# Storing the last 528 columns of the last tile in fifteen partition blocks of falling size

## Chip, cores, metric

One core of a Trainium2 chip runs the kernel. The metric is the device time of one execution in microseconds (us). A profiled execution also has a span, from its first to its last instruction, which is some 1.8 us shorter than the time; all points in time below count from the start of the span.

## The reference

```
x: (8, 4096, 2112) float32
pooled    = x.reshape(8, 1024, 4, 2112).mean(axis=2)
upsampled = repeat(pooled, 4, axis=1)
return x - upsampled
```

Every group of four neighbouring rows loses its mean. 277 MB are read and 277 MB written.

## The kernel before

A tile is 128 groups: 128 partitions with 4 x 2112 = 8448 columns of float32, so 33,792 B per partition. There are n = 64 tiles and six slots of buffer. SyncE issues the loads, VectorE does three adds and one fused multiply-add, ACT issues the stores.

```
for k in range(n):
    b, lap = k % SLOTS, k // SLOTS
    ...
    load = nc.sync.dma_start(out=slots[b][:], in_=xg[tile_rows])
    if lap:
        load._wait_ge(store_sems[b], 16 * lap)
    load.then_inc(load_sems[b], 16)
    ...                                   # three adds into s, then rows += -1/4 * s
    store = nc.scalar.dma_start(out=og[tile_rows], in_=slots[b][:])
    store._wait_ge(done_sem, done)
    store.then_inc(store_sems[b], 16)

for b in range(SLOTS):
    nc.sync.wait_ge(store_sems[b], 16 * len(range(b, n, SLOTS)))
```

Each of the 128 DMAs of this kernel leaves sixteen packets of 4 bytes (2048 in all), one at the end of its rows on each of the sixteen DMA engines; I call them *closing packets*. The semaphore of the last tile's slot shows 176 updates for its eleven stores, sixteen each, so a closing packet adds one. I call the moment at which the semaphore shows it the *increment*: the last closing packet comes at 1282.991 us, its increment at 1283.337. The two are recorded apart.

## Time and profile before

| | before |
|---|---|
| time | 1286.78 us (1286.73 to 1287.18, 6 runs) |
| span | 1285.0 us |
| VectorE busy | 1026.5 us, 80% |
| moved | 553.67 MB, 431 GB/s over the span |
| last store: issued / last closing packet / last increment | 1269.60 / 1282.99 / 1283.34 us |

From the page of the kernel before, the DMA queues (packets, MB, share of sixteen engines) and the issues (KB each, median us to landing):

```profile
q1 hardware_dynamic: 9216, 276.83, 50.0%
q10 hardware_dynamic: 9216, 276.83, 49.9%
q14 instruction: 2, 0.02, 0.0%
...
slot<-in_x_dram SPq DMA_DIRECT2D x64, 4224.0 KB, 59.7
out_dram<-slot ACTq DMA_DIRECT2D x64, 4224.0 KB, 43.9
```

Queue q1 carries the loads, q10 the stores. Most of a store's life here is spent in the queue: it takes 10.0 us of the engines' time (eight rows of 1247 ns on each) and lands 43.9 us after its issue (median).

### The profile page before, as it was taken

To read this page: it belongs to the slowest core of one execution; us is meant where nothing else is said; L and a number is where in the kernel's file an instruction comes from. 1 tells how busy PE (TensorE), PEld (TensorE's weight loads), DVE (VectorE), ACT (ScalarE), POOL (GpSimd) and SP (SyncE) were. 2 spreads that over 40 slices of the span, in tenths; PEclk is the share of its full clock that TensorE was granted. 3 is DMA by queue.
4 is the path that set the end of the run, shared out by engine and by line. 5 is a ranking of instruction groups with operands and counts; after the bars stand their busy time and mean duration, and the time that the engine had idled before them with its cause. 6 is when DMAs were issued, how large, how long until landed. Compare 5 with 4: busy or idle time off the path is not lost.

```text
span 1285.0 us, 439 instructions
## 1 busy us (share of the span) xinstructions
DVE 1026.5 (80%) x256; POOL 0.2 (0%) x4
## 2 busy tenths in 40 slices
DVE  5998778787787877878778788787887878878774
POOL 0000000000000000000000000000000000000000
DMA  9999999999999999999999999999999999999998
GB/s 404 421 438 432 426 438 437 430 429 437 437 431 429 437 437 431 429 437 437 431 429 437 437 431 429 437 436 430 430 438 434 429 432 438 434 428 433 438 434 374
DMA packets 18434, 553.67 MB, mean 431 GB/s; under 512 B 2048, under 2 KB 2048, under 8 KB 2048
## 3 DMA queue, kind: packets, MB, share of 16 engines
q1 hardware_dynamic: 9216, 276.83, 50.0%
q10 hardware_dynamic: 9216, 276.83, 49.9%
q14 instruction: 2, 0.02, 0.0%
HBM read 276.82 MB, written 276.82 MB: 431 GB/s over the span
## 4 chain that ended last, share of the span: by engine, by line
DVE 80%; another core or an unknown queue 17%; DMA 1%; issue 0%; SPq 0%
DVE slot L75 45%; DVE s_ps L71 12%; DVE s_sb L71 12%; DVE s_ps L66 6%; DVE s_sb L66 6%; DMA slot<-in_x_dram 1%; SPq L118 0%; SPq L53 0%
## 5 line engine op out<-in xcount | busy, mean ns | idle before, releaser
L75 DVE SCALAR_TENSOR_TENSOR slot<-s_sb,slot 128x8448 f32<-128x8448 f32 x32 | 286.7, 8958 | 1.1
L75 DVE SCALAR_TENSOR_TENSOR slot<-s_ps,slot 128x8448 f32<-128x8448 f32 x32 | 286.6, 8957 | 1.1
L66 DVE TENSOR_TENSOR s_sb<-slot 128x2112 f32<-128x2112 f32 x32 | 75.5, 2358 | 123.4 <-DMA slot<-in_x_dram 123.4
L66 DVE TENSOR_TENSOR s_ps<-slot 128x2112 f32<-128x2112 f32 x32 | 75.7, 2367 | 113.0 <-DMA slot<-in_x_dram 113.0
L71 DVE TENSOR_TENSOR s_ps<-s_ps,slot 128x2112 f32<-128x2112 f32 x64 | 151.4, 2366 | 2.2
L71 DVE TENSOR_TENSOR s_sb<-s_sb,slot 128x2112 f32<-128x2112 f32 x64 | 150.9, 2358 | 2.2
L107 POOL MEMSET const-uint8-127<- 128x1 uint8 x1 | 0.1, 102 | 0.0
L107 POOL MEMSET const-bfloat16-1.0<- 128x1 bf16 x1 | 0.1, 101 | 0.0
L107 POOL MEMSET const-float32-0.0<- 128x1 f32 x1 | 0.1, 98 | 0.2 <-issue 0.2
L107 POOL MEMSET const-float32-1.0<- 128x1 f32 x1 | 0.1, 98 | 0.0
## 6 DMA issues: line engine op xcount, KB each, us to landing
slot<-in_x_dram SPq DMA_DIRECT2D x64, 4224.0 KB, 59.7
out_dram<-slot ACTq DMA_DIRECT2D x64, 4224.0 KB, 43.9
```

Source lines behind the costliest of these rows:

```text
L66: add = nc.vector.tensor_add(out=s[:], in0=rows[:, 0, :], in1=rows[:, 1, :])
L71: add = nc.vector.tensor_add(out=s[:], in0=s[:], in1=rows[:, f, :])
L75: sub = nc.vector.scalar_tensor_tensor(out=rows, in0=s[:, None, :].to_broadcast([P, STRIDE, D]), scalar=-1.0 / STRIDE, in1=rows, op0=mybir ...
L107: nc = _bacc.Bacc("TRN2", target_bir_lowering=False, num_devices=1)
```

## The change

The intent is to balance the sixteen DMA engines at the end: a block of s < 16 partitions is meant to put one row on each of the first s engines, so blocks of falling size give the first engines more short rows than the last. That the engines are taken in a fixed order is an assumption, and the trace doesn't number them. I count them in that order: engine j is the one that a block of j + 1 partitions reaches and a block of j does not.

```diff
+EDGE = 528
+BLOCKS = (15, 14, 13, 12, 11, 10, 9, 9, 8, 7, 6, 5, 4, 3, 2)
...
-            store = nc.scalar.dma_start(out=og[tile_rows], in_=slots[b][:])
+            split = W - EDGE if k == n - 1 else W
+            store = nc.scalar.dma_start(
+                out=og[tile_rows, :split], in_=slots[b][:, :split]
+            )
...
-        for b in range(SLOTS):
-            nc.sync.wait_ge(store_sems[b], 16 * len(range(b, n, SLOTS)))
+        last = (n - 1) % SLOTS
+        p0 = 0
+        for size in BLOCKS:
+            store = nc.scalar.dma_start(
+                out=og[G - P + p0:G - P + p0 + size, W - EDGE:],
+                in_=slots[last][p0:p0 + size, W - EDGE:],
+            )
+            store.then_inc(store_sems[last], 16)
+            p0 += size
+        assert p0 == P
+
+        for k in range(n - SLOTS, n):
+            extra = len(BLOCKS) if k == n - 1 else 0
+            nc.sync.wait_ge(store_sems[k % SLOTS], 16 * (k // SLOTS + 1 + extra))
```

## The prediction

> **What bounds the kernel now.** I read the page first, for the engine that is full. Columns of the slice view: each digit is the busy share of one fortieth of the span.
>
> ```profile
> DVE 1026.5 (80%) x256; POOL 0.2 (0%) x4
> ...
> DMA  9999999999999999999999999999999999999998
> GB/s 404 421 438 432 426 438 437 430 429 437 437 431 429 437 437 431 429 437 437 431 429 437 437 431 429 437 436 430 430 438 434 429 432 438 434 428 433 438 434 374
> ...
> HBM read 276.82 MB, written 276.82 MB: 431 GB/s over the span
> ```
>
> The DMA row is full from the first slice to the last, VectorE is idle a fifth of the time. So the sixteen DMA engines bound the kernel, and only the last slice (374 GB/s) has room. The waits agree: VectorE waits for loads alone, and SyncE, which issues the loads, waits for stores (first answer VectorE's, second SyncE's):
>
> ```profile
> DVE s_sb L66 <- DMA slot<-in_x_dram: 123.4, 30, 13.3
> DVE s_ps L66 <- DMA slot<-in_x_dram: 113.0, 30, 4.8
> ...
> SPq L61 <- DMA out_dram<-slot: 1170.2, 58, 50.6
> SPq L92 <- DMA out_dram<-slot: 89.3, 1, 89.3
> ```
>
> The last line is the end of the program: SyncE waits 89.3 us for the last store. The change touches that store only, so I cut the tail into windows (us; VectorE busy; POOL; clock; DMA share; GB/s; a packet is counted in the window where it starts):
>
> ```profile
> 1253.00:1270.00 17.00, 16.06 (x4) 0.00 (x0) 1.00 0.97 419
> 1270.00:1280.50 10.50, 0.00 (x0) 0.00 (x0) 1.00 1.06 457
> 1280.50:1281.00 0.50, 0.00 (x0) 0.00 (x0) 1.00 0.16 68
> 1281.00:1281.40 0.40, 0.00 (x0) 0.00 (x0) 1.00 0.01 0
> 1281.40:1281.80 0.40, 0.00 (x0) 0.00 (x0) 1.00 0.21 85
> 1281.80:1283.00 1.20, 0.00 (x0) 0.00 (x0) 1.00 0.00 0
> ```
>
> 85 GB/s over 0.40 us is 34 kB: one row of 33,792 B starts there, and nothing after it. The packet records give the rest: a full row takes an engine 1247 ns from start to start (27.1 GB/s). Fifteen engines write the closing semaphore packet between 1281.200 and 1281.747; the sixteenth starts its last row at 1281.744 and closes at 1282.991. **One engine ends 1.24 us after the next.** The semaphore shows its increment at 1283.337.
>
> Why that one is late is in the records too. The page has two small packets on the instruction queue (q14 instruction: 2, 0.02 MB). They lie at 205.70 and 845.42 us, 8192 B each, and both times the same engine's stream falls back: a 302 ns gap, then a row of 1788 ns instead of 1251, so 0.84 us. Twice that is 1.68 us. On the lists of landings the last of the sixteen lags the fifteenth by about 0.1 us before the first fetch, 0.4 to 0.5 us between them, 1.23 to 1.39 us after the second. 8192 B are 128 instructions [...], and VectorE issues four per tile: 32 tiles at 20 us are the 640 us between the fetches, so I take them for VectorE's instructions. **The trace doesn't number the DMA engines**, so which one this is I can't read from it. The answer hangs on that.
>
> [...] The kernel before has only 128-partition DMAs and sixteen closing packets for each (2048 for 128 DMAs)[...]. [...] The trace shows 8 KiB pieces and that the fetch isn't free for the data.[...] Here the increment shows 0.34 us after the last packet, and rows behind a closing packet start at once[...].
>
> **The change, part by part.** The generated order is the same except for fifteen more DMA issues on the ACT queue and a different order of the closing waits.
>
> 1. The last store loses 528 of 8448 columns: 2112 B a row, by rate 1247 x 2112/33792 = 78 ns. Each engine has eight rows: 0.62 us less on every engine.
> 2. Blocks 15, 14, 13, 12, 11, 10, 9, 9, 8, 7, 6, 5, 4, 3, 2 give engines 0 to 15 this many short rows: 15, 15, 14, 13, 12, 11, 10, 9, 8, 6, 5, 4, 3, 2, 1, 0 (sum 128). A short row is 78 ns, its closing packet about 6 ns (9982 ns between the closing packets of two stores, less 8 x 1247): 84 ns. Net, after step 1: engines 0 and 1 +0.64 us, engine 7 +0.13, engine 8 +0.05, engine 11 -0.29, engine 15 -0.62.
> 3. Fifteen issues more. The first six loads, issued back to back, took 2.94 us, 0.49 each. From 1269.60, sixteen issues take 7.8 us, to 1277.4; the first load's first packet followed its issue by 1.0 us, so the last block is in the rings by 1278.4. The shortened main store frees the first engine at 1281.2 - 0.62 = 1280.6. Hidden, with 2.2 us to spare.
> 4. Closing waits. Before, the wait on the last store stood first: it passed at 1283.354, then three more already satisfied steps to 1283.555. In the changed program its wait stands in the third of four steps, so two of the three are passed early: -0.14 us.
>
> The bulk before 1270 us isn't touched, nor is VectorE. What counts on the path: the latest engine's end, plus step 4.
>
> - The late engine is 15: its end moves to 1282.37; engines 0 and 1, at most 1281.75 + 0.64 = 1282.38. End -0.61, with step 4 -0.75 us: 1286.0.
> - It is 7: +0.13 - 0.14, nothing: 1286.8.
> - It is 0: +0.64 - 0.14 = +0.50: 1287.3.
>
> That is all there is to win or lose by the balance: under 0.06% of the time.
>
> **Rivals.** [...] *Closing packets.* Engine 0 gets fifteen closing packets in 1.3 us. If each had to wait for the one before to be received (0.34 us), that would be 5.1 us, ending at about 1280.8 + 5.1 + 0.35, some 3 us later than now: 1289.5. Against: rows start 6 ns after a closing packet today. *The issue becomes the bound.* If an issue [...] takes over 0.63 us (0.49 plus 2.2/15), the rings run dry before the end; at 0.8 us the last block would come at 1283.4 and the end be about 1 us later. The isolated store issue took 0.338 us, so I doubt it. *An additional instruction fetch.* Fifteen more instructions for ACT could cross a fetch boundary: 0.84 us on one engine. ACT has about 80 instructions and then 97, so a boundary of 128 should not be reached.
>
> **Range and chances.** The design makes sense only if the last engines are late, so I give engine 15 (or near) a little under half, and the rest to middle and first engines. Half at 1286.0 to 1286.6, half at 1286.7 to 1287.8[...]: I choose 1286.8 us, range 1285.9 to 1288.1. The runs before spread 0.45 us, which covers much of it. Two per cent is 25.7 us; no rival comes within a quarter of that. Within 2%: 0.985.
>
> **What would show it right or wrong.** The chain, VectorE's waits and all slices but the last should be as before. ACT's fifteen issues should end before 1279, 0.4 to 0.55 us apart. The tail should hold 256 packets more (128 short rows of 2112 B, 128 closing ones), and the short rows should take near 80 ns; [...] gaps of 0.3 us between them receipts. If the last closing packet belongs to an engine with no short rows, the late engine is 15 and the gain is limited by its own eight rows; if it belongs to one with nine or more, the change loads the engine that was already last. Anything above 1289 would mean that a block's packets don't overlap as I assume.

## The result, and the profile after

The changed kernel takes 1288.47 us (1288.38 to 1288.58, 6 runs) against 1286.78. Ratios here are the mean time of one kernel's runs over that of the other's of the same rounds, so not quite the ratio of the medians: 1.0012, interval 0.9999 to 1.0025. That is the same by the 2% measure, as expected, but 1.7 us longer, and outside the range of 1285.9 to 1288.1. Nearly all runs differ by less than that interval can tell apart, so the argument rests on the packets and semaphore records of the profiled runs, which resolve some 0.01 us, and on medians that agree with them.

From the page of the changed kernel, the bulk is as it was and the last slice is weaker (354 GB/s; 374 before):

```profile
DVE 1026.5 (80%) x256; POOL 0.2 (0%) x4
...
DMA  9999999999999999999999999999999999999998
GB/s 403 420 437 437 431 427 436 437 431 431 434 436 435 431 430 436 437 431 432 433 436 436 430 430 436 437 430 432 433 437 435 430 430 437 437 430 432 433 437 354
...
q10 hardware_dynamic: 9472, 276.83, 49.9%
q14 instruction: 3, 0.02, 0.0%
```

The stores have 256 packets more, the 128 short rows and 128 closing packets that were announced: each row of a block has a closing packet of its own. There is a third instruction fetch (at 1280.905), which I had ruled out. SyncE's waits in the changed kernel (us in total, times, longest):

```profile
SPq L64 <- DMA out_dram<-slot: 1170.2, 58, 50.3
SPq L110 <- DMA out_dram<-slot: 91.0, 3, 69.3
```

The bulk waits 1170.2 us as before; the closing waits grew from 89.3 to 91.0. The fifteen issues on ACT (duration in ns min/median/max, first and last start in us):

```profile
L100 ACTq DMA_DIRECT2D out_dram<-slot x15: 275/693/1232, 1270.0 to 1281.8; - x15
```

They don't end at 1277.4 but past 1281.8: from the third to the ninth, all but one take 1.17 to 1.23 us. The tail of the changed kernel in windows (us; VectorE; POOL; clock; DMA share; GB/s):

```profile
1280.00:1280.50 0.50, 0.00 (x0) 0.00 (x0) 1.00 0.15 63
1280.50:1281.00 0.50, 0.00 (x0) 0.00 (x0) 1.00 0.44 118
1281.00:1281.40 0.40, 0.00 (x0) 0.00 (x0) 1.00 0.93 344
1281.40:1281.80 0.40, 0.00 (x0) 0.00 (x0) 1.00 0.38 127
1281.80:1282.30 0.50, 0.00 (x0) 0.00 (x0) 1.00 0.16 55
1282.30:1283.50 1.20, 0.00 (x0) 0.00 (x0) 1.00 0.10 30
1283.50:1285.10 1.60, 0.00 (x0) 0.00 (x0) 1.00 0.00 0
```

Here two things are new. Between 1282.30 and 1283.50 there is still 30 GB/s: 36 kB, some seventeen short rows. And from 1283.50 on **no data moves at all**, yet the wait passes only at 1285.086: 1.6 us of nothing, where before 0.36 us lay between the last packet and the wait.

The packet records tell whose rows those are. The late engine ends its main rows at 1282.360 (it was 1282.995), then writes thirteen short rows back to back, 88 ns apart, each with a closing packet, the last at 1283.503. Thirteen of the fifteen blocks have four partitions or more. If the engines are taken in a fixed order, the late one is reached by a block of four and not by a block of three: engine number 3. e5, e6 and e10 test that. The increments don't keep that pace. The last ones of the semaphore are:

```
1283.990  1284.170  1284.350  1284.530  1284.710  1284.890  1285.070     every 0.180 us
```

Interleaved with them a second series, which must be another engine's, also steps by 0.18 us and ends earlier, at 1284.716. The late engine's main closing packet of 1282.356 shows at about 1282.73; thirteen increments of 0.180 us behind it make 1285.07. So the difference of the spans, 1286.628 - 1285.031 = 1.597 us, has three parts:

| part | before | after | difference |
|---|---|---|---|
| last closing packet | 1282.991 | 1283.503 | +0.512 |
| from it to its increment | 0.346 | 1.567 | +1.221 |
| from increment to the end of the span | 1.694 | 1.558 | -0.136 |

**Theory.** The late engine's increments come home one in 0.18 us, while it writes a short row in 0.088. The fifteen small DMAs pile up a queue of increments on it, and behind the last store there is no data to hide that queue. What inside the engine takes the 0.18 us no run shows. **Rivals:** the rows themselves (cut, unaligned); the slow issues; the extra instruction fetch; the semaphore that all sixteen stores share.

### The profile page after: what moved, and what is told of

The parts are those of the page before. It is cut to its first block, busy times and chain, and to the rows that moved or that the text cites. A ratio compares the mean times of both kernels' runs of the same rounds, so it can differ in the third digit from the quotient of the medians.

```text
span 1286.6 us, 454 instructions
## 1 busy us (share of the span) xinstructions
DVE 1026.5 (80%) x256; POOL 0.2 (0%) x4
## 4 chain that ended last, share of the span: by engine, by line
DVE 80%; another core or an unknown queue 17%; DMA 1%; issue 0%; SPq 0%
DVE slot L78 45%; DVE s_ps L74 12%; DVE s_sb L74 12%; DVE s_ps L69 6%; DVE s_sb L69 6%; DMA slot<-in_x_dram 1%; SPq L136 0%; SPq L56 0%
```

## The experiments

Each ran five rounds beside the kernel before (four in e8), whose median was 1286.80 to 1286.85 us. Packets are those of the one profiled run; "closing" and "increment" are the last of the last tile's semaphore unless said otherwise.

| run | closing | increment | span | median us |
|---|---|---|---|---|
| before | 1282.991 | 1283.337 | 1285.03 | 1286.8 |
| changed | 1283.503 | 1285.070 | 1286.63 | 1288.47 |
| e1 waits only | 1283.017 | 1283.361 | 1284.92 | 1286.70 |
| e2 one block | 1282.987 | 1283.361 | 1284.92 | 1286.81 |
| e3 blocks early | 1283.864 | 1284.267 | 1285.83 | 1287.65 |
| e4 rows twice as long | 1283.972 | 1284.583 | 1286.14 | 1287.92 |
| e5 blocks of three | odd run, see there | | 1286.79 | 1286.63 |
| e6 blocks of four | 1283.640 | 1284.104 | 1285.85 | 1287.57 |
| e7 more instructions | 1284.289 | 1284.684 | 1286.38 | 1287.89 |
| e9 few closings | 1283.478 | 1283.881 | 1285.4 | 1287.28 |
| e10 own semaphores | 1283.507 | 1285.117 | 1287.0 | 1288.79 |
| e11 wait last | 1282.848 | 1283.189 | 1284.68 | 1286.51 |

**e1, the closing waits alone.**

```diff
-        for b in range(SLOTS):
-            nc.sync.wait_ge(store_sems[b], 16 * len(range(b, n, SLOTS)))
+        for k in range(n - SLOTS, n):
+            nc.sync.wait_ge(store_sems[k % SLOTS], 16 * (k // SLOTS + 1))
```

> The kernel before with only the closing waits in the changed kernel's source order (last store's wait in the third of four steps instead of the first). Theory: no packet moves; the two passed steps are saved, span 0.14 us shorter (1284.9), time about 1286.64. Rival, that the order of the waits is nothing: span 1285.03, time 1286.78.

The deciding wait passed at 1283.378 and the next step, the last, at 1283.443; before, 1283.354 and 1283.555. So 0.136 us are saved, the third row of the table above. The part works as predicted, and the medians (1286.70 and 1286.85) agree.

**e2, one block of all partitions.**

```diff
-BLOCKS = (15, 14, 13, 12, 11, 10, 9, 9, 8, 7, 6, 5, 4, 3, 2)
+BLOCKS = (128,)
```

> The changed kernel with one block of 128 partitions for the 528 columns: the same cut of the rows, sixteen engines with eight short rows each, one closing packet more per engine instead of fifteen. Theory (serial increments of 0.18 us on the late engine are the cost, with its 13 rows): late engine's last closing packet at about 1283.05, its increment 0.35 us later, with the waits' 0.14 us a time of 1286.7, as before. Rival A (cutting the rows short is the cost, or the unaligned short rows): still 1287.5 or more. Rival B (the fifteen issues[...] set the end): gone here too, 1286.7; it is told apart by e3.

The short rows cost next to nothing: the late engine writes eight of them at 82 to 83 ns without closing packets in between, closes at 1282.987 and shows it 0.374 us later. Cutting the store, and the odd start of the short rows, are not the cause.

**e3, the blocks on the last tile but one.**

```diff
-            split = W - EDGE if k == n - 1 else W
+            split = W - EDGE if k == n - 2 else W
...                                     # and the fifteen blocks follow that store
```

> The fifteen blocks on the last tile but one, so their rows load the engines as in the changed kernel, but their closing increments are behind 10 us of the last store's rows. Theory: only the balance is left: engine 3 is late, has 13 short rows of 88 ns (1.14 us) for 0.62 us less of main rows: +0.52, less 0.14 for the waits: span 1285.4, time 1287.15. Rival A (rows [...] cost it all): 1288.4 as changed. Rival B (issue order at the very end): 1286.7, no balance effect.

It lands between theory and rival: 1287.65, not 1287.15. The late engine wrote its thirteen short rows at the usual 88 ns. The one surprise lies behind them: its first two full rows of the last tile took 1616 and 1338 ns instead of 1251, 0.45 us more together, and that tile's last closing packet came at 1283.864 instead of the 1283.503 of the changed kernel (the engine had been 0.09 us ahead before the stretch). On the semaphore of the blocks the increments still came every 0.18 us until 1275.077, 1.65 us after the short rows' last closing packet at 1273.429. The other engines agree: eight of the sixteen show two such stretched rows behind the blocks, 0.32 to 0.67 us together, among them engines with nine, eleven and fifteen short rows, while one with eight short rows writes its first full row in 1251 ns. So most of the queue was hidden behind data here (an increment 1.65 us after its closing packet, 0.45 us of lost time), but it held up the rows behind it. That was missing from my theory, which had it hidden for free.

**e4, rows twice as long.**

```diff
-EDGE = 528
+EDGE = 1056
```

> The changed kernel with twice the columns in the blocks (1056; rows of 4224 B, about 0.165 us with closing packet, still under 0.18). Theory: the end is the late engine's main end plus 13 increments of 0.18 us; the main rows end 0.62 us earlier, so the time is 0.6 us SHORTER than the changed kernel's: span 1286.0, time 1287.85. Rival (rows set the end): 13 rows at 0.165 instead of 0.088 are 1.0 us more, less 0.62: 0.4 us longer, 1288.9.

The kernel that moves twice the data through the unbalanced blocks is **faster** than the changed one, 1287.92 against 1288.47. Tail windows of this run:

```profile
1281.80:1282.30 0.50, 0.00 (x0) 0.00 (x0) 1.00 0.52 194
1282.30:1283.50 1.20, 0.00 (x0) 0.00 (x0) 1.00 0.33 120
1283.50:1285.10 1.60, 0.00 (x0) 0.00 (x0) 1.00 0.03 8
```

Rows are still being written past 1283.50, where the changed kernel moves nothing, and yet the last increment comes 0.49 us sooner. At 0.166 us a row the late engine is now nearly as slow as its increments. The rows as the cause fall. So do the issues: the last block was issued at 1282.60 here, 0.84 us later than in the changed kernel, and the end came earlier.

**e5 and e6, which number the late engine has.**

```diff
-EDGE = 528
+EDGE = 1056
-BLOCKS = (15, 14, 13, 12, 11, 10, 9, 9, 8, 7, 6, 5, 4, 3, 2)
+BLOCKS = (112, 3, 3, 3, 3, 3, 1)        # e5
+BLOCKS = (112, 4, 4, 4, 4)              # e6
```

> Last 1056 columns as blocks of 112, 3, 3, 3, 3, 3, 1 partitions. If a block of k partitions goes to engines 0 to k-1 and the late engine is number 3, it gets 7 rows of 4224 B in one block and no others: it is relieved of one row (0.16 us), two closing packets 1.1 us apart so no backlog: last closing packet 1282.86, span 1284.8, time 1286.5 (0.3 less than before, 0.14 of it by the waits). If the late engine were one of 0 to 2, it would have 5 or 6 rows and increments more: 1287.4 or more.

> The same with blocks of 112, 4, 4, 4, 4. If the late engine is number 3 it has four rows and four increments more than in e5: last increment 1283.2 + 4 x 0.18 = 1283.93, span 1285.5, time 1287.25. If the late engine is number 4 or above, as in e5: 1286.5. Together with e5 this fixes the number.

Four of the five runs of e5 took 1286.54 to 1286.65 us, those of e6 1287.45 to 1287.63 with one outlier of 1289.74. In e6 the last engine to end shows seven rows, a closing packet, and then four rows with four closing packets 166 ns apart; the increments at the very end lie 0.19 to 0.18 us apart. In e5 the last engine has no row behind its seven. So it gets a row from each block of four and none from a block of three: as counted above, it is engine 3. The fifth run of e5, which happens to be the profiled one, took 1288.57: in it three main rows of 29,568 B took 2178, 2021 and 1879 ns instead of 1095, while the other engines were already in the block of 112. Slowed rows on engines other than the late one are in the changed kernel, e4, e6, e9 and e10 too. No run here isolates what slows them, and it stays open.

**e7, more VectorE instructions.**

```diff
+            nc.vector.memset(pad[:, 0:1], 0.0)     # one per tile, before the store
```

> The kernel before with one tiny memset more per tile on VectorE [...]: five instructions a tile, 320 in all. Theory: the late engine is late because it carries VectorE's instruction fetches, one per 128 instructions; a third one comes near 1195 us and the late engine ends 0.84 us later: span 1285.9, time 1287.65. Rival (the lateness is that engine's own, or the fetch goes elsewhere): 1286.8.

Three fetches now lie at 166.0, 680.9 and 1186.1 us. Each is followed by a row of 1788 or 1789 ns, and the lag of the last increment behind the fifteenth is 0.84, 1.68 and 2.76 us right after them (2.34 at the end). The best of the five runs is 1287.64, the median 1287.89, and the profiled run, 1288.16, is the slowest. How much of a fetch shows depends on where the engine stood: when the first one came it was 0.14 us ahead of the last engine in this run, and 0.45 us in that of the kernel before. The lateness is made by VectorE's instruction fetches.

**e8, fewer VectorE instructions (failed).**

```diff
-            add = nc.vector.tensor_add(out=s[:], in0=rows[:, 0, :], in1=rows[:, 1, :])
...                                     # and the two adds behind it; for k < n - 2:
+            add = nc.vector.tensor_reduce(out=s[:], in_=rows.rearrange("p f d -> p d f"),
+                                          op=mybir.AluOpType.add, axis=mybir.AxisListType.X)
```

> The kernel before with the three adds of a tile replaced by one reduction over the four rows (about 8.8 us estimated from the 8.96 us of the other instruction with as many elements, instead of 7.1), all but the last two tiles: 132 VectorE instructions instead of 256. Theory: one fetch less, late engine ends 0.84 us earlier, still last by 0.4: span 1284.2, time 1285.95. Rival (no cause in the fetches): 1286.8. Should the reduction take over 11 us, VectorE becomes the bound and the time is far longer.

The single reduction took twice the time of the three adds, and VectorE became the bound: 1508.53 us. From its page:

```profile
DVE 1478.0 (98%) x132; POOL 0.2 (0%) x4
...
L67 DVE TENSOR_REDUCE s_sb<-slot 128x2112 f32<-128x8448 f32 x31 | 447.7, 14441 | 13.5 <-DMA slot<-in_x_dram 13.5
```

14.44 us for one reduction, where I had estimated 8.8 from an instruction with as many elements. The trace has one fetch on q14 instead of two, as it should, but says nothing on the end. Whether a kernel with one fetch gains 0.84 us was not shown.

**e9, the same rows on engine 3 with two closing packets.** The blocks of 100 and 27 partitions are meant to give engine 3 its thirteen short rows as 10 + 3; the trace shows that they do.

```diff
-BLOCKS = (15, 14, 13, 12, 11, 10, 9, 9, 8, 7, 6, 5, 4, 3, 2)
+BLOCKS = (100, 27, 1)
```

> The changed kernel with blocks of 100, 27 and 1 partitions. [...] engine 3 has the same 13 short rows as in the changed kernel, but two closing packets for them instead of 13. Theory (increments queue up on the late engine): 13 rows at 0.083 us without a queue, last closing packet 1283.45, increment 0.35 later, waits 0.14 less: span 1285.35, time 1287.1. Rival (the rows on engine 3 are the cost, however they are closed): 1288.4 as changed.

This is the direct test. The late engine writes ten rows 82 ns apart, a closing packet, three rows, a closing packet at 1283.478: within 0.03 us of the changed kernel's. Its tail windows:

```profile
1281.80:1282.30 0.50, 0.00 (x0) 0.00 (x0) 1.00 0.12 46
1282.30:1283.50 1.20, 0.00 (x0) 0.00 (x0) 1.00 0.08 32
1283.50:1285.10 1.60, 0.00 (x0) 0.00 (x0) 1.00 0.00 0
```

The data ends as in the changed kernel (0.08 against 0.10 of sixteen engines, then nothing), but the increment comes 0.403 us later instead of 1.567. The time is 1287.28: of the 1.7 us, 1.2 are gone with eleven closing packets on that engine, and no row was moved from it. The edit also drops twelve issues, and with them the third instruction fetch. Neither made the 1.2 us: in the changed kernel the last block was issued by 1282.03, before the late engine had ended its main rows, and e3 has the third fetch too (at 1257.489, on another engine, which it cost 0.42 us: a gap of 0.31 us, then a row of 1367 ns) while its last increment comes 0.40 us after the closing packet.

**e10, a semaphore for each block.**

```diff
+    edge_sems = [tc.alloc_semaphore(f"edge{i}") for i in range(len(BLOCKS))]
...
-            store.then_inc(store_sems[last], 16)
+            store.then_inc(edge_sems[i], 16)
...
+        for i in range(len(BLOCKS)):
+            nc.sync.wait_ge(edge_sems[i], 16)
```

> The changed kernel with a semaphore of its own for each block. If the 0.18 us between increments belong to the DMA engine, they stay, and the closing waits are two steps longer behind the deciding one (0.13 us): time 1288.6. If they belong to the one semaphore that all increment, the increments come 0.35 us after each row and the time falls to 1287.2 to 1287.4.

The last increments of the thirteen first blocks' semaphores come at 1282.899, 1283.097, 1283.293 and so on to 1285.117, 0.18 to 0.20 us apart, though each goes to another semaphore. The block of three partitions is not in that series, which gives engine 3 a third time. Each block's semaphore gets as many increments from engines as the block has partitions, 15 down to 2. So it is the engine that spaces them, not the shared semaphore. The time is 1288.79.

**e11, the deciding wait on the last step.**

```diff
+        last = (n - 1) % SLOTS
+        for b in [last] + [b for b in range(SLOTS) if b != last]:
-        for b in range(SLOTS):
             nc.sync.wait_ge(store_sems[b], 16 * len(range(b, n, SLOTS)))
```

> The kernel before with the wait on the last store in the last of the four closing steps. Theory: 0.2 us less than before (all three passed steps saved; 0.06 less than e1): span 1284.83, time 1286.6. Rival (order of waits is nothing): 1286.8.

1286.51 us (1286.46 to 1286.95) against 1286.82: the fastest version by median, ahead of both kernels, though the ratio of 0.9998 (0.9986 to 1.0011) doesn't separate it from before. By the records the order is worth 0.2 us: the deciding step is the last (1283.205, 0.016 after the increment, where before 0.218 lay between). The rest of its profiled span comes from a closing packet that was 0.14 us earlier by itself.

## Why the prediction was wrong

- **The bound, the late engine and its cause: right.** The DMA engines bound the kernel, one is 1.24 us late, and e7 shows that the fetches of VectorE's instructions make it so.
- **Step 1 (the main rows) and step 4 (the waits): right**, with 1282.995 to 1282.360 (0.635 for 0.62) and 0.136 us.
- **Step 2, the cost of a short row: the term that was mis-sized.** "A short row is 78 ns, its closing packet about 6 ns" is right for the data, 88 ns. But the kernel ends with the increments, not with the rows, and there each of the thirteen costs 0.18 us. For engine 3 the prediction's own sum would have been -0.62 + 13 x 0.084 = +0.47, less 0.14: 1287.1, inside the range. Nearly all of what is missing, 1.22 us by the records, is the queue of increments, and e9 takes it away while the rows stay.
- **The rival that came closest was dropped on the wrong evidence.** "Closing packets" had the mechanism with 0.34 us each, so 5.1 us for fifteen. The argument against it, that rows start 6 ns after a closing packet, is true even now; it shows that the engine goes on, not that the increment has arrived. A latency of 0.34 us for one says nothing on how many can follow each other. Nor would the sign that it named, gaps between the short rows, have shown the queue: there are none on the late engine.
- **Which engine is late: left open, guessed as the last.** It is number 3 (e5, e6, e10), which the falling blocks load with five rows more than it had. The change puts weight on the engine that was already last.
- **Step 3, the issues: wrong in size, harmless.** 12.1 us for the fifteen, not 7.4; e4 shows that they don't set the end. What paces them is open: in e3, where more rows were queued ahead of them, the same fifteen issues took 0.28 to 0.39 us each after two of 0.94 and 1.01, so full queues alone don't explain it.
- **The extra fetch: wrongly ruled out, harmless.** It came at 1280.905, and the late engine's rows show no gap there. Seven issues more bring it (e5), five don't (e6).
- **Slowed rows: none on the changed kernel's late engine**, all of whose thirteen short rows are 86 ns. Other engines were slowed: two of their main rows took 1.31 and 1.46 us instead of 1.17, and thirteen of their short rows 0.09 to 0.47 us. They ended before the late engine, so it cost nothing here. The cause is open, as for the odd run of e5.

## What to carry to other kernels

The wait on a store passes when its semaphore shows it, and in these runs the increments of one engine have a rate of their own: 0.18 to 0.20 us each (changed kernel, e6, e10), where a short row with its closing packet takes 0.088. So at the end of a kernel like this one, count the closing packets per engine, not only the bytes, and use few DMAs with many rows rather than many with one: two closing packets for the thirteen rows instead of thirteen took 1.2 us off (e9). Before balancing engines, find out which one is late and why; here it was the one that carries VectorE's instruction fetches, 0.84 us each, and the blocks reached it with more work. A queue that no data hides belongs in the working even where each member of it looks free.
